# A one-core encoder layer with product-key experts: late picks for two tiles, a pinned row in the gather ring, and pools laid out from both ends

## The chip, the cores and the metric

The kernel runs on one core of a Trainium2 chip. Its engines are TensorE (PE in the rows), VectorE (DVE), ScalarE (ACT) and GpSimd (POOL); SyncE (SP) issues the plain DMAs, and GpSimd the gathers. Each engine works through its own instructions in their order. The metric is the device time of one execution in microseconds. Before the change it is 2861.89 us, the median of three runs (2860.47 to 2866.61).

## The reference

One layer over 1024 tokens of 1024 features: a token mixer, a layer of product-key experts, and a gated embedding. The change touches the experts (`P` is 128):

```python
def peer(n, w_q, sub_keys, expert_u, expert_v):
    q = (nf @ w_q).reshape(t, PEER_HEADS, D_KEY)             # 8 heads of 256
    s1 = jnp.einsum("thd,hkd->thk", q1, sub_keys[:, 0])      # 128 scores a side
    s2 = jnp.einsum("thd,hkd->thk", q2, sub_keys[:, 1])
    v1, i1 = lax.top_k(s1, TOPK)                             # 16 of 128
    v2, i2 = lax.top_k(s2, TOPK)
    cand = (v1[..., :, None] + v2[..., None, :]).reshape(t, PEER_HEADS, TOPK * TOPK)
    vals, ci = lax.top_k(cand, TOPK)
    idx = (e1 * N_KEYS + e2)                                 # 128 picks a token
    gates = jax.nn.softmax(vals, axis=-1)
    ...
        ug = expert_u[ib]                                    # 16384 experts of 1024
        act = jax.nn.gelu(jnp.einsum("td,tkd->tk", xb, ug)) * gb
        vg = expert_v[ib]
        return jnp.einsum("tk,tkd->td", act, vg)
h = h + peer(rmsnorm(h, g_ffn), ...)
gate = jax.nn.sigmoid(rmsnorm(h, g_ple) @ w_pg)
h = h + (p @ w_pe) * gate
return rmsnorm(h, g_final)
```

## The kernel before

The 1024 tokens are 8 tiles of 128. The **front** takes them in four pairs: the mixer (`mix_in`, `mix_out`), then `choose` (L283), which makes the queries and the scores of each head on TensorE, copies the scores with ScalarE, and has VectorE look for the 16 best (`top16`, L328, five instructions over 128 columns) and combine the two sides (`select`, L336: eight searches over 80 candidates, then one-hots over 1024 columns to read the keys). Between the heads `fill` (L319) takes the next pieces of the gate tables.

The experts are worked out in two ways. Tiles 1 to 4 (`DENSE`) go through all 16384 experts: `gate_table` (L395) turns picks and gates into a table of one gate per token and expert, by one-hots on VectorE, GpSimd and ScalarE and matmuls, and stores it to DRAM (`Wd`). The **dense stage** (`dense`, L436) then goes through 128 blocks of 128 experts: loads of u, v and the table's columns on SP; ScalarE rounds u and v to a short form (`uh`, `vh`), GpSimd makes the rest (`ul`, L470, `vl`, L477); 24 matmuls for z (L481 to L483); gelu; VectorE multiplies by the table (L486); three matmuls per output group and a sum on VectorE (L504 to L508). Tiles 5 to 7 (`GATHER`) fetch just the 128 picked rows of each token by indirect DMA: `u_step` (L524) gathers rows of expert_u (L536) into a ring of tiles `g`, and VectorE makes a dot with each (L538); `v_step` (L555) gathers rows of expert_v and adds them, weighted, to `accP` (L568). One step is 32 rows. Tile 0 (`MIXED`) has its u side gathered in the front and its v side in the dense stage, so it has a gate table too, made from its acts. One more step of 32, of tile 5, runs in the front (`UE`); the other gathers run beside and after the dense stage. The **back** (`back_in`, `back_out`) ends the layer tile by tile.

A scheduler sorts the instructions of all these loops into one order per engine from its own estimate of their times. Where a tile lies in SBUF is set by pools: the front's pools are closed at L641, and the dense stage's pools take over their space, tile by tile, as their last readers finish.

Four places matter here. `UAT, GAT` (L59) say after which pair tile 0's gathers and its table are put into the program: after the pair that begins with tile 6, the last one. `FG` is the front's ring of three `g` tiles; the normalized row that the dots are made with is a tile `hrow` of its own (L527). `choose` finds the picks of all eight tiles in the front. And `u`, `uh`, `ul` (pool `du`) lay in space that the gathers of the front didn't use.

Of the kernel before, what the change touches and what calls it, by code (L numbers as in the profile page):

```python
# [26 lines left out]
def trunk(ctx: ExitStack, tc: tile.TileContext, x, pT, w_inF, w_inV, chan, ln_c, w_sT, b_s, w_out, g_row,  # L27
# [7 lines left out]
    def row_const(pool, name, src, i, n):  # L35
# [23 lines left out]
    UAT, GAT, RATE = 6, 6, 3  # L59
# [7 lines left out]

    UE, WR = 1, 8
# [5 lines left out]
    nTd = dram.tile([P, 8, NA * P], F32, name="nTd")  # L74
    TG = 32
# [9 lines left out]
    wbp = fctx.enter_context(tc.tile_pool(name="wbp", bufs=2))  # L85
    psum = fctx.enter_context(tc.tile_pool(name="psum", bufs=2, space=bass.MemoryType.PSUM))

# [4 lines left out]
    iotaP = psum.tile([P, P], F32, name="iotaP", bufs=1)  # L92
# [190 lines left out]
    def choose(t0, nt, nT):  # L283
# [3 lines left out]
        for t in range(nt):  # L287
            tv = work.tile([P, 2, NH, K], F32, name="tv")
            ti = work.tile([P, 2, NH, K], U32, name="ti")
            top.append((tv, ti))  # L290
        for h in range(NH):
# [36 lines left out]
    def top16(v, i, s):  # L328
        nc.vector.max(v[:, 0:8], s)
        nc.vector.max_index(i[:, 0:8], v[:, 0:8], s)  # L330
        s2 = work.tile([P, s.shape[1]], F32, name="s2", bufs=4)
# [4 lines left out]
    def select(t, tv, ti):  # L336

        cand = work.tile([P, NH, 80], F32, name="cand", bufs=1)
        v1, v2 = tv[:, 0], tv[:, 1]
        nc.vector.tensor_add(cand[:, :, 0:16], v1[:, :, 0:1].to_broadcast([P, NH, 16]), v2)  # L340
        nc.vector.tensor_add(cand[:, :, 16:72].rearrange("p h (i j) -> p h i j", i=7),
                             v1[:, :, 1:8, None].to_broadcast([P, NH, 7, 8]),
                             v2[:, :, None, 0:8].to_broadcast([P, NH, 7, 8]))
        nc.vector.tensor_add(cand[:, :, 72:80], v1[:, :, 8:16], v2[:, :, 0:1].to_broadcast([P, NH, 8]))
        vals = work.tile([P, NH, K], F32, name="vals")
        pos = work.tile([P, NH, K], U32, name="pos")
        for h in range(NH):
            top16(vals[:, h], pos[:, h], cand[:, h])

        f = work.tile([P, 5, NH * K], BF, name="pf")  # L350
        p_ = pos.rearrange("p h k -> p (h k)")
        sh = work.tile([P, NH * K], U32, name="sh")
# [4 lines left out]
        ib = work.tile([P, 2, NH * K], BF, name="ib")  # L357
# [6 lines left out]
        own = work if t in GATHER else wbp  # L364
        e = own.tile([P, 2, NH * K], F32, name="e", bufs=2 if t in GATHER else 5)
        for side in range(2):
            for h0 in range(0, NH, HB):

                c = slice(h0 * K, (h0 + HB) * K)
                tb = work.tile([P, K, HB, K], BF, name="tb", bufs=1)  # L370
                nc.scalar.copy(tb, ti[:, side, h0:h0 + HB].rearrange("p h i -> p i h")[:, :, :, None]
                               .to_broadcast([P, K, HB, K]))
                oh = work.tile([P, K, HB * K], BF, name="oh", bufs=2)
                nc.vector.tensor_tensor(oh, iota16, ib[:, side, None, c].to_broadcast([P, K, HB * K]), op=OP.is_equal)
# [20 lines left out]
    def gate_table(t):  # L395
# [4 lines left out]
        pe = psum.tile([P, 4, P], F32, name="gt", bufs=3)  # L400
# [7 lines left out]
        for g in range(P // TG):  # L408
            st = wbp.tile([P, P, TG], F32, name="st")
            for q in range(0, TG, 4):  # L410
# [17 lines left out]
                pw = psum.tile([P, P, 4], F32, name="gt", bufs=3)  # L428
# [7 lines left out]
    def dense():  # L436
# [12 lines left out]
        def u_stage(b):  # L449
            if b % NG == 0:  # L450
# [4 lines left out]
                wm = dm.tile([P, P // TG, NG, TG], F32, name="wm")  # L455
# [94 lines left out]
    def experts(tiles):  # L550
# [185 lines left out]
```

## Time and profile before

| | us |
|---|---|
| median of three runs | 2861.89 |
| profiled execution | 2862.61 |
| its span | 2860.8 |
| PE, DVE, POOL, ACT busy | 2620.5, 2156.9, 1945.5, 1007.6 |
| last gate matmul of the front ends | 1084.29 |
| first matmul of the dense stage | 1086.52 |
| last gathered row added | 2830.14 |

The span is divided by the seam at 1086 us. Left of it all engines share the work and none is full; right of it PE is nearly full until the dense blocks end at about 2722 us, and from there to the end the last gathers and the back's matmuls run side by side. Matmuls are pipelined, so the busy time of PE is not matmuls times their mean. An idle time in square brackets is what the engine waited before that row, with what ended it.

### The profile page before, as it was taken

How to read it: one execution, taken by the hardware profiler on the slowest of the kernel's cores; microseconds unless marked ns; L12 is line 12 of the kernel's file. 1: busy time of each engine (PE TensorE's matmuls, PEld its weight loads, DVE VectorE, ACT ScalarE, POOL GpSimd, SP SyncE). 2: the span in 40 equal slices, each digit the busy share in tenths (PEclk: the TensorE clock that was granted, in tenths of full speed). 3: DMA queues.
4: the chain of work that ended last, by engine and by line, in shares of the span. 5: the costliest groups of instructions: out<-in, count | busy, mean ns of one | idle time of the engine just before them, and what ended most of it. 6: DMA issues, size and time to landing. Idle time of an engine off the chain costs nothing.

```text
span 2860.8 us, 37645 instructions
## 1 busy us (share of the span) xinstructions
PE 2620.5 (92%) x12671; PEld 2203.2 (77%) x12671; DVE 2156.9 (75%) x4738; ACT 1007.6 (35%) x1930; POOL 1945.5 (68%) x1740
## 2 busy tenths in 40 slices
PE   7998999889678678999999999999999999999988
PEld 6887888688677656888787888878787788788767
DVE  5567888999977886777777777777777777677776
ACT  3312455335764544222322223232222322222342
POOL 0000377347876787888878888888887878888773
PEclk9998999899789779999999999999999999999999
DMA  6353688787657649899999999999999999999885
GB/s 203 129 185 120 236 300 301 242 304 253 221 206 274 228 184 339 317 324 344 331 333 328 331 347 330 338 329 342 325 336 329 328 348 332 335 339 324 299 290 174
DMA packets 299698, 820.92 MB, mean 287 GB/s; under 512 B 26096, under 2 KB 117616, under 8 KB 296944
## 3 DMA queue, kind: packets, MB, share of 16 engines
q0 software_dynamic: 129024, 469.82, 45.8%
q1 hardware_dynamic: 170480, 348.70, 35.6%
q8 instruction: 100, 1.64, 0.2%
q14 instruction: 94, 0.77, 0.1%
HBM read 764.93 MB, written 53.48 MB: 286 GB/s over the span
## 4 chain that ended last, share of the span: by engine, by line
PE 33%; DMA 23%; DVE 17%; POOL 13%; issue 10%; ACT 2%; SPq 0%; POOLq 0%; DVEq 0%; ACTq 0%
DMA g<-expert_u,idx 10%; DMA g<-expert_v,idx 10%; PE z L158 4%; DVE g L538 4%; POOL g L536 4%; PE mm L612 3%; POOL vl L477 3%; PE mm L504 3%; PE z L481 3%; PE z L482 3%; PE mm L505 3%; PE mm L506 3%; PE z L483 3%; PE mm L299 2%; PE mm L267 2%
## 5 line engine op out<-in xcount | busy, mean ns | idle before, releaser
L536 POOL DMA_INDIRECT g<-expert_u,idx x512 | 511.9, 1000 | 369.6 <-DVE g L538 163.2
L568 DVE SCALAR_TENSOR_TENSOR accP<-g,act,accP 128x1024 f32<-128x1024 f32 x384 | 493.2, 1284 | 210.9 <-DMA g<-expert_v,idx 207.4
L538 DVE SCALAR_TENSOR_TENSOR g<-g,nP 128x1024 f32<-128x1024 f32 x352 | 422.8, 1215 | 178.5 <-DMA g<-expert_u,idx 177.1
L566 POOL DMA_INDIRECT g<-expert_v,idx x384 | 367.7, 957 | 144.4 <-DVE accP L568 60.7
L504 PE MATMUL mm<-vh,ah 128*128 128x512 f32 x1024 | 400.3, 392 | 13.5 <-DVE accA L508 6.8
L481 PE MATMUL z<-nh,uh 128*128 128x512 f32 x1024 | 401.8, 393 | 8.1 <-DVE al L490 5.9
L482 PE MATMUL z<-nl,uh 128*128 128x512 f32 x1024 | 400.6, 391 | 2.0 <-DVE nl L446 2.0
L483 PE MATMUL z<-nh,ul 128*128 128x512 f32 x1024 | 400.2, 391 | 0.0
L505 PE MATMUL mm<-vl,ah 128*128 128x512 f32 x1024 | 399.2, 391 | 0.0
L506 PE MATMUL mm<-vh,al 128*128 128x512 f32 x1024 | 396.7, 390 | 0.0
L421 POOL TENSOR_SCALAR oh<-iota,eT,gT 128x128 f32<-128x128 f32 x320 | 314.5, 991 | 63.9 <-PE gt L430 50.8
L468 ACT CAST uh<-u 128x1024 fp32r<-128x1024 f32 x128 | 134.8, 1053 | 574.8 <-PE z L482 459.3
L477 POOL TENSOR_TENSOR vl<-v,vh 128x512 fp32r<-128x512 f32 x256 | 328.2, 1302 | 3.2 <-ACT vh L475 0.7
L470 POOL TENSOR_TENSOR ul<-u,uh 128x1024 fp32r<-128x1024 f32 x128 | 309.3, 2417 | 6.9 <-ACT uh L468 4.6
L430 PE MATMUL gt<-oh,oh 128*128 128x128 f32 x1280 | 221.4, 321 | 95.1 <-POOL oh L421 40.4
L430 PEld LDWEIGHTS gt<-oh,oh 128*128 128x128 f32 x1280 | 194.5, 224 | 123.1 <-POOL oh L421 82.6
L475 ACT CAST vh<-v 128x512 fp32r<-128x512 f32 x256 | 153.1, 621 | 306.9 <-DMA v<-expert_v 250.6
L538 DVE SCALAR_TENSOR_TENSOR g<-g,hrow 128x1024 f32<-128x1024 f32 x160 | 197.3, 1236 | 72.3 <-DMA g<-expert_u,idx 72.2
L158 PE MATMUL z<-aT,w 128*128 128x256 f32 x960 | 227.0, 393 | 16.0 <-DMA w<-w_inF 13.1
L299 PE MATMUL mm<-nT,w 128*128 128x256 f32 x1024 | 237.0, 383 | 4.4 <-DMA w<-w_q 4.4
L508 DVE TENSOR_TENSOR accA<-mm,accA 128x512 f32<-128x512 f32 x320 | 217.8, 684 | 27.0 <-PE mm L506 26.7
L504 PEld LDWEIGHTS mm<-vh,ah 128*128 128x128 f32 x1024 | 193.0, 189 | 56.7 <-DVE accA L508 9.8
(368 smaller groups left out, 4586.6 us busy)
## 6 DMA issues: line engine op xcount, KB each, us to landing
u<-expert_uT SPq DMA_DIRECT2D x128, 512.0 KB, 6.4
v<-expert_v SPq DMA_DIRECT2D x128, 512.0 KB, 4.9
Wd<-st SPq DMA_DIRECT2D x20, 2048.0 KB, 8.4
w<-w_q SPq DMA_DIRECT2D x64, 512.0 KB, 4.8
w<-Wd SPq DMA_DIRECT2D x128, 256.0 KB, 9.7
w<-w_inF SPq DMA_DIRECT2D x60, 512.0 KB, 3.6
wo<-w_out SPq DMA_DIRECT2D x32, 512.0 KB, 4.5
g<-expert_u,idx POOLq DMA_INDIRECT x512, 6.3
```

Of the source, the lines that this page charges most:

```text
L430: nc.tensor.matmul(pw[:, :, k], oh2[:, k], oh1[:, k], start=True, stop=True)
L477: nc.gpsimd.tensor_tensor(vl, v[:, s * 512:s * 512 + 512], vh.bitcast(F32), op=OP.subtract)
L481: nc.tensor.matmul(ph, uh[:, c], nh[:, c], start=c == 0, stop=False)
L482: nc.tensor.matmul(ph, uh[:, c], nl[:, c], start=False, stop=False)
L483: nc.tensor.matmul(ph, ul[:, c], nh[:, c], start=False, stop=c == 7)
L504: nc.tensor.matmul(po, ah[:, c], vh, start=i == 0, stop=False)
L505: nc.tensor.matmul(po, ah[:, c], vl, start=False, stop=False)
L506: nc.tensor.matmul(po, al[:, c], vh, start=False, stop=i == NG - 1)
L536: nc.gpsimd.indirect_dma_start(out=ug, out_offset=None, in_=expert_u, in_offset=bass.IndirectOffsetOnAxis(ap=idx[:, k:k + 1], axis=0))
L538: nc.vector.scalar_tensor_tensor(ug, ug, 1.0, ns[t, front], op0=OP.mult, op1=OP.mult, accum_out=dots[:, k - b * KB:k - b * KB + 1])
L566: nc.gpsimd.indirect_dma_start(out=vg, out_offset=None, in_=expert_v, in_offset=bass.IndirectOffsetOnAxis(ap=idx[:, kk:kk + 1], axis=0))
L568: nc.vector.scalar_tensor_tensor(acc, vg, act[:, k:k + 1], acc, op0=OP.mult, op1=OP.add)
```

## The change

Seven edits belong together. (1) For tiles 6 and 7 (`LATE`) `choose` only stores the scores to DRAM (`sd`, 16 stores of 128 KB). `choose_late` loads them again, head by head into one buffer, and does searches and `select` on VectorE; it is called in `experts` ahead of the second steps of tiles 5 and 6. There the one-hots of `select` go over 256 columns in 16 rounds instead of 1024 in 4. (2) Tile 0's gathers and its table are put into the program after pair 3 (tiles 4 and 5) instead of pair 4. (3) The row h of the gathers has no tile of its own any more; it takes one of the `g` tiles and, in the front, holds it for as long as its tile's dots last. (4) `wbp`, `hold`, `gath`, `dm` and the new pool `late` are laid out from the right end of SBUF, the others from the left. The dense stage's `uh`, `ul` and the first `w` now lie over the front's `g` tiles. (5) `cand` is made for four heads at a time. (6) `wm` has one buffer instead of two. (7) The dense pools close after the expert steps instead of ahead of them, and the gate tables' PSUM is a pool of its own.

```diff
-    UAT, GAT, RATE = 6, 6, 3
+    UAT, GAT, RATE = 4, 4, 3
...
+    LATE = (6, 7)
...
+    sd = {t: dram.tile([P, NH, 2, P], F32, name=f"sd{t}") for t in LATE}
...
-    wbp = fctx.enter_context(tc.tile_pool(name="wbp", bufs=2))
+    wbp = fctx.enter_context(tc.tile_pool(name="wbp", bufs=2, side="right"))
...
             for t in range(nt):
+                if t0 + t in LATE:
+                    nc.sync.dma_start(sd[t0 + t][:, h], s[:, t])
+                    continue
                 tv, ti = top[t]
...
-            picks[t0 + t] = select(t0 + t, *top[t])
-
+            if t0 + t not in LATE:
+                picks[t0 + t] = select(t0 + t, *top[t])
+
+    def choose_late(t):
+
+        top = top_tiles()
+        for h in range(NH):
+            s = sel.pool.tile([P, 2, P], F32, name="s")
+            nc.sync.dma_start(s, sd[t][:, h])
+            for side in range(2):
+                top16(top[0][:, side, h], top[1][:, side, h], s[:, side])
+        picks[t] = select(t, *top)
...
+    class Sel:
+
+        def __init__(self, pool, heads, bufs):
+            self.pool, self.heads, self.bufs = pool, heads, bufs
+            self.iota = (pool if bufs else fconst).tile([P, K, heads * K], BF, name="iota16", bufs=1)
...
+    sel = Sel(work, 4, None)
...
-                wm = dm.tile([P, P // TG, NG, TG], F32, name="wm")
+                wm = dm.tile([P, P // TG, NG, TG], F32, name="wm", bufs=1)
...
-            h = gath.tile([P, D], F32, name="hrow", bufs=1)
+            h = gath.tile([P, D], F32, name="g")
...
         prev = None
+        late = list(LATE)
         for st in steps:
+            if late and st[1] == 1:
+                choose_late(late.pop(0))
             if st not in acts:
...
-    hold = ctx.enter_context(tc.tile_pool(name="hold", bufs=1, reuse_waits="tile"))
-    gath = ctx.enter_context(tc.tile_pool(name="gath", bufs=BG, reuse_waits="tile"))
+    hold = ctx.enter_context(tc.tile_pool(name="hold", bufs=1, side="right", reuse_waits="tile"))
+    gath = ctx.enter_context(tc.tile_pool(name="gath", bufs=BG, side="right", reuse_waits="tile"))
...
-    dm = dctx.enter_context(tc.tile_pool(name="dm", bufs=2, reuse_waits="tile"))
+    dm = dctx.enter_context(tc.tile_pool(name="dm", bufs=2, side="right", reuse_waits="tile"))
+    late = dctx.enter_context(tc.tile_pool(name="late", bufs=1, side="right", reuse_waits="tile"))
+    sel = Sel(late, 1, 1)
     dense()
+    h_last = experts(GATHER)
     dctx.close()
-    h_last = experts(GATHER)
```

What the scheduler makes of it shows at three places at the seam. GpSimd before, the first two `ul` (L470), among the gate one-hots (L421) of tile 4:

```order
L421 TENSOR_SCALAR oh2_6679<-iota_122,eT_6333,gT_6332 128x128 [waits PE_49]
L421 TENSOR_SCALAR oh2_6679<-iota_122,eT_6333,gT_6332 128x128 x3
L470 TENSOR_TENSOR ul_8718<-u_8714,uh_8716 128x1024 [waits DMAHW4_49,DMAHW3_49,DMAHW5_49,DMAHW2_49,DMAHW6_49,DMAHW1_49,DMAHW7_49,DMAHW0_49,Activation_49]
L470 TENSOR_TENSOR ul_8765<-u_8761,uh_8763 128x1024 [waits DMAHW2_49,DMAHW1_49,DMAHW4_49,DMAHW0_49,Activation_49]
L421 TENSOR_SCALAR oh2_6709<-iota_122,eT_6333,gT_6332 128x128 [waits PE_49]
L421 TENSOR_SCALAR oh2_6709<-iota_122,eT_6333,gT_6332 128x128 x3
```

GpSimd after, the same two (L499 now; L565 is a gather, `g_19525` and above are those of tile 5's second step):

```order
L565 DMA g_19567<-expert_u,idx_5826 128x1024 [waits DMASW6_49,DVE_49]
L576 TENSOR_TENSOR act_8245<-act_8245,gate_5819 128x32 [waits Activation_49]
L565 DMA g_19570<-expert_u,idx_5826 128x1024 [waits DMASW7_49,DVE_49]
L565 DMA g_19573<-expert_u,idx_5826 128x1024 [waits DMASW0_49,DVE_49]
L565 DMA g_19576<-expert_u,idx_5826 128x1024 [waits DMASW1_49,DVE_49]
L565 DMA g_19579<-expert_u,idx_5826 128x1024 [waits DMASW2_49,DVE_49]
L565 DMA g_19582<-expert_u,idx_5826 128x1024 [waits DMASW3_49,DVE_49]
L499 TENSOR_TENSOR ul_8347<-u_8343,uh_8345 128x1024 [waits DMAHW3_49,Activation_49]
L565 DMA g_19585<-expert_u,idx_5826 128x1024 [waits DMASW4_49,DVE_49]
L499 TENSOR_TENSOR ul_8394<-u_8390,uh_8392 128x1024 [waits DMAHW4_49,Activation_49]
```

The first `ul` has moved behind the last gate one-hot and 28 gathers that follow it.

SP before, the first loads of the table's columns (`w`, L453) and of u (L466), among the query weights `w3`:

```order
L453 DMA w_8703<-Wd1_92 128x4x128 [waits DMAHW2_49,DMAHW5_49,DMAHW0_49,PE_49]
L453 DMA w_8703<-Wd2_93 128x4x128
L453 DMA w_8703<-Wd3_94 128x4x128
L466 DMA u_8714<-expert_uT 128x1024
L466 DMA u_8761<-expert_uT 128x1024
L453 DMA w_8902<-Wd1_92 128x4x128 [waits DMAHW3_49,DMAHW1_49]
L453 DMA w_8902<-Wd2_93 128x4x128
L453 DMA w_8902<-Wd3_94 128x4x128
L434 DMA Wd4_95<-st_6484 128x4096 [waits DMAHW4_49,Activation_49]
```

SP after (L482 and L495 now; L325 are the score loads of tile 6's pick, L485 and L501 the loads of `wm` and v):

```order
L485 DMA wm_8536<-Wd0_98 128x4x128 [waits DMAHW6_49,DMAHW3_49,Pool_49]
L325 DMA s_19224<-sd6_92 128x256 [waits DMAHW4_49,DMAHW0_49,DVE_49]
L485 DMA wm_8875<-Wd0_98 128x4x128 [waits DMAHW5_49,DMAHW3_49,Pool_49]
L325 DMA s_19238<-sd6_92 128x256 [waits DMAHW4_49,DVE_49]
L482 DMA w_8332<-Wd1_94 128x4x128 [waits DMAHW7_49,DVE_49]
L482 DMA w_8332<-Wd2_95 128x4x128
L482 DMA w_8332<-Wd3_96 128x4x128 [waits DMAHW1_49]
L482 DMA w_8332<-Wd4_97 128x4x128 [waits DMAHW2_49]
L495 DMA u_8343<-expert_uT 128x1024
L495 DMA u_8390<-expert_uT 128x1024
```

The u loads stand behind score loads that wait on VectorE, and behind a `w` load that waits on it too.

VectorE before, what follows the last gate one-hot (L423): the lower part of the tokens (`nl`, L446) and the first dots of tile 5's second step:

```order
L423 TENSOR_SCALAR oh2_8509<-iotaP_124,eT_8088,gT_8087 128x128 [waits Pool_49]
L423 TENSOR_SCALAR oh2_8509<-iotaP_124,eT_8088,gT_8087 128x128 x3
L531 TENSOR_TENSOR nP_19559<-nP_19559,g_ffn_77 128x1024 [waits Activation_49]
L446 TENSOR_TENSOR nl_8670<-al_8671,nh_8669 128x512 [waits DMAHW4_49,Activation_49]
L446 TENSOR_TENSOR nl_8670<-ah_8675,nh_8669 128x512 [waits DMAHW5_49,Activation_49]
L538 SCALAR_TENSOR_TENSOR g_19563,dots_19562<-g_19563,nP_19559 128x1024 [waits DMASW0_49,DVE_49]
L538 SCALAR_TENSOR_TENSOR g_19566,dots_19562<-g_19566,nP_19559 128x1024 [waits DMASW1_49]
L538 SCALAR_TENSOR_TENSOR g_19569,dots_19562<-g_19569,nP_19559 128x1024 [waits DMASW2_49]
```

VectorE after, some 50 rows behind the last gate one-hot (L357 to L362 are the searches, L372 and L375 `cand`, L567 the dots; `g_8242` is the last gather of tile 5's front step):

```order
L358 MAX_INDEX ti_19181<-tv_19180,s_19224 128x8 [waits DVE_49]
L372 TENSOR_TENSOR cand_19296<-tv_19180 128x4x56
L567 SCALAR_TENSOR_TENSOR g_8239,dots_8148<-g_8239,g_8144 128x1024 [waits DMASW7_49]
L361 MAX tv_19180<-s2_19228 128x8 [waits DVE_49]
L362 MAX_INDEX ti_19181<-tv_19180,s2_19228 128x8 [waits DVE_49]
L375 TENSOR_TENSOR cand_19296<-tv_19180 128x4x8
L567 SCALAR_TENSOR_TENSOR g_19552,dots_19524<-g_19552,nP_19521 128x1024 [waits DMASW0_49]
L360 MATCH_REPLACE s2_19234<-tv_19180,s_19224 128x128 [waits DVE_49]
L567 SCALAR_TENSOR_TENSOR g_8242,dots_8148<-g_8242,g_8144 128x1024 [waits DMASW1_49]
L361 MAX tv_19180<-s2_19234 128x8 [waits DVE_49]
L567 SCALAR_TENSOR_TENSOR g_19555,dots_19524<-g_19555,nP_19521 128x1024 [waits DMASW2_49]
```

The dots of the front's last step now stand between the searches of tile 6's pick; from the last one-hot to `g_8242` there are 18 dots and nearly four heads.

## Rows read from the trace of the kernel before

**Rows 1.** The page, busy us of an engine, its share of the span, instructions.

```profile
PE 2620.5 (92%) x12671; PEld 2203.2 (77%) x12671; DVE 2156.9 (75%) x4738; ACT 1007.6 (35%) x1930; POOL 1945.5 (68%) x1740
```

**Rows 2.** Stretches: busy us (instructions) by engine; PE clock, DMA share, GB/s.

```profile
500.00:600.00 100.00, 83.95 (x470) 71.76 (x470) 92.83 (x337) 31.53 (x58) 33.09 (x31) 0.86 0.78 265
700.00:800.00 100.00, 76.90 (x494) 69.55 (x493) 94.89 (x369) 67.22 (x162) 82.69 (x78) 0.85 0.68 236
840.00:1086.00 246.00, 183.52 (x957) 159.22 (x955) 190.41 (x687) 130.38 (x302) 181.26 (x192) 0.82 0.62 224
1086.00:1546.00 460.00, 444.89 (x1910) 364.54 (x1911) 332.67 (x452) 134.33 (x208) 373.07 (x311) 0.97 0.95 334
...
2724.00:2861.00 137.00, 118.41 (x523) 96.01 (x521) 98.44 (x103) 46.94 (x81) 76.98 (x89) 0.94 0.66 227
```

**Rows 3.** DVE lines kept apart by shape: as section 5 of the page.

```profile
L330 DVE FIND_INDEX8 ti<-tv,s 128x8 uint32<-128x128 f32 x128 | 35.9, 282 | 0.0
...
L332 DVE MATCH_REPLACE8 s<-tv,s 128x128 f32<-128x128 f32 x128 | 34.9, 273 | 0.0
...
L374 DVE TENSOR_TENSOR oh<-iota,ib 128x1024 bf16<-128x1024 bf16 x32 | 21.7, 688 | 0.0
...
L330 DVE FIND_INDEX8 pos<-vals,cand 128x8 uint32<-128x80 f32 x64 | 14.4, 231 | 0.0
...
L330 DVE MATCH_VALUE_LOAD ti<-tv,s 128x8 f32 x128 | 9.8, 76 | 0.0
```

**Rows 4.** Section 5 of the page: group | busy us, mean ns | idle.

```profile
L538 DVE SCALAR_TENSOR_TENSOR g<-g,hrow 128x1024 f32<-128x1024 f32 x160 | 197.3, 1236 | 72.3 <-DMA g<-expert_u,idx 72.2
```

**Rows 5.** POOL in time, 562 to 600 us: start, length, row, [idle, releaser].

```profile
562.40 1.94 POOL L536 DMA_INDIRECT g<-expert_u,idx  x1 [0.15 <-DVE s L332]
...
600.05 1.15 POOL L536 DMA_INDIRECT g<-expert_u,idx  x1 [0.84 <-DVE g L538]
```

**Rows 6.** POOL in time, 820 to 980 us.

```profile
826.44 0.28 POOL L547 TENSOR_TENSOR wm<-wm,gate 128x32 f32<-128x32 f32 x1
...
839.14 0.56 POOL L122 TENSOR_TENSOR rB<-ss,half 128x1 f32<-128x1 f32 x1 [1.46 <-DVE ss L119]
...
847.72 1.07 POOL L536 DMA_INDIRECT g<-expert_u,idx  x1 [1.85 <-DVE idx L392]
...
968.69 1.03 POOL L536 DMA_INDIRECT g<-expert_u,idx  x1 [0.17 <-issue]
...
978.04 5.64 POOL L470 TENSOR_TENSOR ul<-u,uh 128x1024 fp32r<-128x1024 f32 x2
```

**Rows 7.** PE in time, end of the front and first dense blocks.

```profile
1082.34 1.95 PE L430 MATMUL gt<-oh,oh 128*128 128x128 f32 x14 [0.37 <-DVE oh L423]
1086.52 0.73 PE L481 MATMUL z<-nh,uh 128*128 128x512 f32 x2 [2.23 <-ACT nh L445]
...
1109.63 1.22 PE L504 MATMUL mm<-vh,ah 128*128 128x512 f32 x2 [6.55 <-ACT vh L475]
```

**Rows 8.** The page, sections 5 and 6 (issues: count, KB each, us to landing).

```profile
L421 POOL TENSOR_SCALAR oh<-iota,eT,gT 128x128 f32<-128x128 f32 x320 | 314.5, 991 | 63.9 <-PE gt L430 50.8
L468 ACT CAST uh<-u 128x1024 fp32r<-128x1024 f32 x128 | 134.8, 1053 | 574.8 <-PE z L482 459.3
...
L470 POOL TENSOR_TENSOR ul<-u,uh 128x1024 fp32r<-128x1024 f32 x128 | 309.3, 2417 | 6.9 <-ACT uh L468 4.6
...
u<-expert_uT SPq DMA_DIRECT2D x128, 512.0 KB, 6.4
```

**Rows 9.** The chain of waits, 840 to 1130 us: start, length, what.

```profile
1093.04 15.90 DMA v<-expert_v
```

**Rows 10.** POOL lines of 2724 to 2861 us.

```profile
L566 POOL DMA_INDIRECT g<-expert_v,idx x43 | 45.0, 1046 | 23.2 <-DVE accP L568 16.3 <-issue 6.0 <-DVE sg L620 0.6
```

**Rows 11.** DVE in time, end of the gathers.

```profile
2828.86 1.28 DVE L568 SCALAR_TENSOR_TENSOR accP<-g,act,accP 128x1024 f32<-128x1024 f32 x1
```

**Rows 12.** PE in time, transposes of the last tile.

```profile
2836.08 1.03 PE L594 MATMUL z<-ident,a 128*128 128x128 f32 x8
```

More of the change, by code (lines that the diff above doesn't have):

```diff
@@ L287, in choose @@
         for t in range(nt):
-            tv = work.tile([P, 2, NH, K], F32, name="tv")
-            ti = work.tile([P, 2, NH, K], U32, name="ti")
-            top.append((tv, ti))
+            if t0 + t not in LATE:
+                top.append(top_tiles())
         for h in range(NH):
@@ L314, in choose, with top_tiles, tile @@
         for t in range(nt):
[L315 removed]
+            if t0 + t not in LATE:
+                picks[t0 + t] = select(t0 + t, *top[t])
[7 more added lines that the diff above has]
+        picks[t] = select(t, *top)
+    def top_tiles():
+        return sel.tile([P, 2, NH, K], F32, "tv"), sel.tile([P, 2, NH, K], U32, "ti")
+    class Sel:
+        def __init__(self, pool, heads, bufs):
+            self.pool, self.heads, self.bufs = pool, heads, bufs
+            self.iota = (pool if bufs else fconst).tile([P, K, heads * K], BF, name="iota16", bufs=1)
+            nc.gpsimd.iota(self.iota, pattern=[[1, K], [0, heads * K]], base=0, channel_multiplier=0,
+                           allow_small_or_imprecise_dtypes=True)
+        def tile(self, shape, dt, name, bufs=2):
+            return self.pool.tile(shape, dt, name=name, bufs=self.bufs or bufs)
+    sel = Sel(work, 4, None)
     filler, n_gt = [], [0]
@@ L330, in top16 @@
         nc.vector.max_index(i[:, 0:8], v[:, 0:8], s)
-        s2 = work.tile([P, s.shape[1]], F32, name="s2", bufs=4)
+        s2 = sel.tile([P, s.shape[1]], F32, "s2", 4)
         nc.vector.match_replace(s2, v[:, 0:8], s, NEG)
@@ L336, in select @@
     def select(t, tv, ti):
[L338 to L350, printed above, removed]
+        vals = sel.tile([P, NH, K], F32, "vals")
+        pos = sel.tile([P, NH, K], U32, "pos")
+        for h0 in range(0, NH, 4):
+            cand = sel.tile([P, 4, 80], F32, "cand")
+            v1, v2 = tv[:, 0, h0:h0 + 4], tv[:, 1, h0:h0 + 4]
+            nc.vector.tensor_add(cand[:, :, 0:16], v1[:, :, 0:1].to_broadcast([P, 4, 16]), v2)
+            nc.vector.tensor_add(cand[:, :, 16:72].rearrange("p h (i j) -> p h i j", i=7),
+                                 v1[:, :, 1:8, None].to_broadcast([P, 4, 7, 8]),
+                                 v2[:, :, None, 0:8].to_broadcast([P, 4, 7, 8]))
+            nc.vector.tensor_add(cand[:, :, 72:80], v1[:, :, 8:16], v2[:, :, 0:1].to_broadcast([P, 4, 8]))
+            for h in range(4):
+                top16(vals[:, h0 + h], pos[:, h0 + h], cand[:, h])
+        f = sel.tile([P, 5, NH * K], BF, "pf")
         p_ = pos.rearrange("p h k -> p (h k)")
-        sh = work.tile([P, NH * K], U32, name="sh")
+        sh = sel.tile([P, NH * K], U32, "sh")
         nc.vector.tensor_scalar(sh, p_, 3, None, op0=OP.logical_shift_right)
@@ L356, in select @@
         nc.vector.scalar_tensor_tensor(f[:, 1], f[:, 0], -64.0, f[:, 1], op0=OP.add, op1=OP.max)
-        ib = work.tile([P, 2, NH * K], BF, name="ib")
+        ib = sel.tile([P, 2, NH * K], BF, "ib")
         nc.vector.tensor_copy(ib[:, 0], f[:, 1])
@@ L363, in select @@
         nc.vector.tensor_add(ib[:, 1], f[:, 4], f[:, 3])
-        own = work if t in GATHER else wbp
-        e = own.tile([P, 2, NH * K], F32, name="e", bufs=2 if t in GATHER else 5)
+        e = sel.tile([P, 2, NH * K], F32, "e") if t in GATHER else wbp.tile([P, 2, NH * K], F32, name="e", bufs=5)
+        HB = sel.heads
         for side in range(2):
@@ L556, in v_step @@
             if b == 0:
-                h = gath.tile([P, D], F32, name="hrow", bufs=1)
+                h = gath.tile([P, D], F32, name="g")
                 nc.sync.dma_start(h, h1d[t])
@@ L569, in v_step @@
             if b == P // KB - 1:
-                h = gath.tile([P, D], F32, name="hrow", bufs=1)
+                h = gath.tile([P, D], F32, name="g")
                 nc.scalar.copy(h, acc)
```

19 lines of the change are left out of this document (8 added, 11 removed).

## The prediction

> **What bounds the kernel now.** I read the summary of engines first, then busy time by stretch, then single engines in order of time around the seams. TensorE is busy 92% of the span [rows 1], but not evenly. In the dense stage it has little to give: 444.89 of 460 us from 1086 to 1546, with VectorE at 332.67 [rows 2]. So the dense stage ends when TensorE has done its matmuls, and whatever moves its start moves the end. The front is another matter. At 500 to 600 and 700 to 800 us VectorE is busy 92.83 and 94.89 us of 100, TensorE only 83.95 and 76.90 [rows 2]: there the picks, the one-hots and the gathered dots on VectorE are late. From 840 to 1086 VectorE has 190.41 of 246 us and TensorE 183.52, at a granted clock of 0.82 [rows 2]; neither is full. The profiled run took 2862.61 us, 1.8 more than its span of 2860.8 and 0.7 more than the median of 2861.89. The sum is made against the profiled run.
>
> **What leaves the front.** A pick of one tile is 16 searches over 128 columns and 8 over 80. A search has five instructions of 273 to 282 ns and three value loads of 76 [rows 3], 1.61 us; over 80 columns five of 231 and the loads, 1.38. That is 16 × 1.61 + 8 × 1.38 = 36.8 us. The one-hot part has eight passes at 688 ns [rows 3], 5.5 us, and halvings, which I estimate at 4.5 more: 47 us a tile, 94 for both, gone from VectorE in the front. How much of it shows depends on what is late next. Two things replace it: the matmuls of pair 4 and of the gate tables, which stay, and the ring of gathers. The ring still has three slots, but now the pinned row h sits in one: two are free. With three, 14 gathers from 562.40 to 600.05 [rows 5] make 13 intervals of 2.90 us, a slot's round being 8.69 us (issue, landing, dot, and the wait for VectorE to come to it). With two the same round gives one gather per 4.34 us.
>
> I take the last piece of the front, from pair 4's norm to the last gate matmul. Before, it runs from 839.14 + 0.56 [rows 6] to 1082.34 + 1.95 [rows 7], 244.6 us. After, GpSimd's order has 33 groups of gate one-hots and 47 gathers there (before 38 and 32). By the ring 47 × 4.34 = 204 us. By GpSimd alone 33 × 4 × 0.991 [rows 8] + 47 × 1.05 (1.03 to 1.07 [rows 6]) = 180. The later of the two holds: 244.6 − 204 = **−40 us**, from −64 (GpSimd alone) to 0 (the ring also delays what stands before it; the earlier pairs I take as unmoved, since they lose dots and get a slower ring).
>
> **What the seam costs.** Before, the first two lower parts of u, `ul`, were made at 978.04 us [rows 6], a hundred us ahead of their matmuls, and TensorE went from the last gate matmul to the first dense one with 2.23 us idle; one more wait, 6.55 us for vh at 1109.63, followed [rows 7]. After, `uh`, `ul` and the first w lie over the slots of the front's ring. The first w load waits on VectorE, the first u load stands behind it on SP's queue, and on GpSimd 28 gathers stand between the last gate one-hot and the first `ul`. What they all wait for is VectorE: between its last one-hot and the last dot of tile 5's front step it has 18 dots and four heads of tile 6's pick. 18 × 1.236 [rows 4] + 4 × 2 × 1.61 = 35 us, with two small adds 36. Behind that come the u load 6.4, the cast 1.053 and the subtraction 2.417 [rows 8]: 9.9. At a VectorE that never waits the gap is 46 us. From 840 to 1086 it was busy 77% (190.41 of 246), and here it waits for landings again, and for the score loads, which share one buffer: 36 / 0.77 = 47, the gap 57. Two waits of before, 2.23 + 6.55, fall inside. Added: **+48 us**. Below: 46 − 8.8 = +37. Above: a busy share of 0.6 and a first load as slow as the first v, 15.90 us [rows 9]: 60 + 19.4 − 8.8 = +71. The gap can't hide: both products of a block need `uh`, the third needs `ul`, and no gate matmuls are left.
>
> **What the dense stage takes up.** The two picks become 94 us plus about 8 for the one-hot passes in eighths instead of halves, over the first 460 us, where VectorE had 460 − 332.67 = 127 us free [rows 2]. It would be busy at 435 of 460, 94%. That is the load of 700 to 800 us, where TensorE lost much; but there its matmuls were fed by VectorE directly, and here two buffers of z lie between. From 0 (127 is more than 102) to 60 (TensorE at 83.95 of 100, the 500 to 600 row, instead of 96.7: 13% of 460). I take a third, **+20 us**, nearer to the row of the same stage.
>
> Here the Trainium skill has a rule that speaks against the change. The row: GpSimd is busy 373.07 of the 460 us [rows 2], 87 free. The rule (SBUF — State Buffer, Who interferes with whom): a VectorE instruction with two inputs in SBUF and a GpSimd instruction that reads SBUF shut each other out for a whole instruction. The searches' replacing and index steps have two such inputs, as do `ul` and `vl`. If a quarter of the 102 us fell on GpSimd's work, some 25 of its 87 free us would go; it would still keep up, so by that rule the sum stays, with less room. No row here shows such a block apart.
>
> **The end.** Ten more gathers of the expert steps are placed ahead of the last dense blocks: 49 are left after it instead of 59. In 2724 to 2861 us GpSimd spent 45.0 + 23.2 us on 43 [rows 10], 1.6 each: 16 us. But TensorE's own back is nearly as late: the last gather is added at 2828.86 + 1.28 [rows 11] and the last tile's transposes start at 2836.08 [rows 12]. Half of it: **−8 us**, from −16 to 0.
>
> **Sum.** 2862.6 − 40 + 48 + 20 − 8 = 2882.6; less the 0.7 to the median, **2882 us**.
>
> **Rivals.**
> 1. *VectorE alone was late in the front.* Two slots are enough, since a slot's round shrinks when VectorE comes to it sooner, and all 94 us go. For it: 94.89 of 100 at 700 to 800 us [rows 2]. Against: from 840 on, where most of tile 7's pick stood, VectorE had 55 us idle. 2862 − 94 + 48 + 20 − 8 = 2828. It decides from a round of 7 us (47 × 3.5 = 165).
> 2. *The ring takes the whole gain.* Rounds of two slots hold the 128 gathers of tile 0 as well, and pair 4 starts later by what its own stretch saves. For it: 2.90 against 4.34 us. Against: tile 0's acts, done at 826.44 [rows 6], took longer per gather than that before too. 0 + 48 + 20 − 8: 2922.
> 3. *The picks slow every block.* VectorE at 94% holds TensorE as in the front: +60 for +20, 2922. For it: the rows of 500 to 800 us. Against: the free 127 us.
> 4. *The terms cancel*, with a seam of 37 us and +5 in the dense stage: −40 + 37 + 5 − 4 = −2, 2860.
>
> The change does what it says in each: the order has the searches behind the last one-hot.
>
> **How the numbers follow.** My forecast has 40%, with its own range from 2868 to 2905. Rival 1 has 28%, rival 2 13%, rival 3 9%, rival 4 10%. This kernel's times tell 0.2%, 5.7 us, from no change. Faster: rival 1, 28%. Within: rival 4, 10%. Slower: 40 + 13 + 9 = 62%. The range of 2830 to 2928 leaves out the lower half of rival 1 and a few in a hundred above.
>
> **What would show it.** Right: a TensorE idle time near 50 us, released by GpSimd's `ul`, ahead of the first dense product; GpSimd's gathers of tile 0 at over 4 us each; VectorE at over 90% from the seam on for about 400 us; the front's last gate matmul at 1030 to 1055. Wrong: that matmul before 1010 (rival 1) or after 1075 (rival 2), a seam under 20 us, or a dense stage whose TensorE is busy under 90% in its first 460 us (rival 3).

## The result

The changed kernel takes 2985.52 us (median of four runs, 2978.71 to 2992.45) against 2861.18: a ratio of 1.0431, interval 1.0403 to 1.0459. The forecast was 2882 with a range up to 2928: the sign was right and the size was not. The profiled execution took 2992.45 us, its span is 2990.7. Where the 130 us between the two spans went:

| | before | after | difference | forecast |
|---|---|---|---|---|
| last gate matmul ends | 1084.3 | 1088.0 | +3.7 | −40 |
| from there to the first dense matmul | 2.2 | 75.6 | +73.3 | +55 |
| dense stage, first to last matmul | 1636.3 | 1693.9 | +57.6 | +13 |
| from there to the last row of VectorE | 134.3 | 129.6 | −4.7 | −8 |

(The forecast's +48 for the seam is split here into the gap, 57 us instead of 2.2, and the 6.6 us wait for vh, which lay behind the first dense matmul.)

Busy time by stretch of the changed kernel (columns as in [rows 2]; the last two stretches begin at its first dense matmul and at the end of its dense stage):

```profile
500.00:600.00 100.00, 79.65 (x464) 68.98 (x465) 94.54 (x336) 36.98 (x70) 30.20 (x30) 0.91 0.72 237
700.00:800.00 100.00, 76.60 (x451) 67.50 (x450) 84.92 (x332) 65.33 (x156) 75.15 (x74) 0.86 0.59 206
840.00:1088.00 248.00, 171.66 (x894) 151.41 (x894) 130.78 (x247) 107.71 (x256) 177.16 (x185) 0.82 0.63 225
1163.60:1623.60 460.00, 412.94 (x1701) 330.48 (x1702) 431.27 (x887) 125.06 (x203) 320.16 (x265) 0.95 0.85 286
2857.50:2991.00 133.50, 119.08 (x536) 97.00 (x534) 86.85 (x93) 46.87 (x81) 66.00 (x80) 0.95 0.56 199
```

From 840 to 1088 us VectorE has lost 60 us of work and stands idle almost half of the time; GpSimd works about as much as before, TensorE 12 us less [rows 2], and the stretch is no shorter. In the dense stage VectorE comes to 431 of 460 us (435 were forecast, but by other terms, see below), and TensorE falls from 444.89 [rows 2] to 412.94.

GpSimd in time: the gathers of tile 0 on their own (answering [rows 5]), and its last act (answering [rows 6]).

```profile
562.42 0.94 POOL L565 DMA_INDIRECT g<-expert_u,idx  x1 [4.64 <-DVE g L567]
...
590.55 0.94 POOL L565 DMA_INDIRECT g<-expert_u,idx  x1 [2.86 <-DVE g L567]
...
959.53 0.62 POOL L576 TENSOR_TENSOR wm<-wm,gate 128x32 f32<-128x32 f32 x1
```

Between the first two rows lie eight intervals, 3.52 us each: two free slots, so a round of 7.0. Over all 128 gathers of tile 0 it is 4.96 us (before 3.92), and the last act comes at 959.53 instead of 826.44. Between pair 4's norm and the last gate matmul there are 46 gathers 5.32 us apart, a round of 10.6. They reach from end to end of the stretch, but that alone does not show that the ring sets its length: before, with three slots, 37 gathers lay 5.62 us apart there.

TensorE at the seam (answering [rows 7]):

```profile
1084.22 3.82 PE L459 MATMUL gt<-oh,oh 128*128 128x128 f32 x16 [3.50 <-POOL oh L450]
1163.59 0.79 PE L510 MATMUL z<-nh,uh 128*128 128x512 f32 x1 [75.55 <-ACT uh L497]
```

What the 75.55 us consist of shows on three engines in time. VectorE (L567 are the dots; L560 makes the row for tile 5's second step):

```profile
1089.70 1.97 DVE L567 SCALAR_TENSOR_TENSOR g<-g 128x1024 f32<-128x1024 f32 x1 [3.75 <-DMA g<-expert_u,idx]
...
1104.62 4.77 DVE L567 SCALAR_TENSOR_TENSOR g<-g 128x1024 f32<-128x1024 f32 x1 [8.29 <-DMA g<-expert_u,idx]
...
1120.99 1.23 DVE L560 TENSOR_TENSOR nP<-nP,g_ffn 128x1024 f32<-128x1024 f32 x1 [8.70 <-ACT nP L559]
...
1144.75 1.22 DVE L567 SCALAR_TENSOR_TENSOR g<-g 128x1024 f32<-128x1024 f32 x1
```

SP (L482 and L495 are the loads of `w` and u):

```profile
1144.86 0.34 SPq L325 DMA_DIRECT2D s<-sd  x1
1146.00 2.69 SPq L482 DMA_DIRECT2D w<-Wd  x4
1148.74 2.96 SPq L495 DMA_DIRECT2D u<-expert_uT  x2
```

ScalarE, the rounding of u (L497):

```profile
1162.49 1.04 ACT L497 CAST uh<-u 128x1024 fp32r<-128x1024 f32 x1 [16.25 <-DMA u<-expert_uT]
```

The last dot of tile 5's front step ends at 1145.97 us. Three hundredths later SP issues the `w` load, behind it u; u lands 13.7 us later (its median before was 6.4 [rows 8]), and only then `uh` starts. The links forecast for the gap are all there but one (`uh` ends it, and `ul` costs 1.22 us more behind it); the waits in them were longer.

What TensorE waited for in the first 460 us of the dense stage, first after (engine, tile, line <- releaser: us, times, longest):

```profile
PE mm L533 <- DVE accA L537: 41.8, 20, 4.8
PE mm L533 <- ACT ah L517: 1.9, 2, 1.1
```

And the same before:

```profile
PE mm L504 <- DVE accA L508: 6.0, 3, 2.2
```

TensorE waits for VectorE to add a finished output group, and the late picks stand ahead of that addition. The longest of these waits stand behind one-hot passes of `select` that took several times their usual time. One shape of them, in the front before (first row) and in those 460 us after:

```profile
L377 DVE TENSOR_TENSOR oh<-oh 128x128 bf16<-128x128 bf16 x32 | 7.1, 221 | 0.2
L406 DVE TENSOR_TENSOR oh<-oh 128x128 bf16<-128x128 bf16 x30 | 20.9, 697 | 0.5
```

And the longest of TensorE's waits, with two such passes ahead of the addition and what GpSimd did meanwhile:

```profile
1286.47 2.36 POOL L499 TENSOR_TENSOR ul<-u,uh 128x1024 fp32r<-128x1024 f32 x1
1286.56 2.37 DVE L406 TENSOR_TENSOR oh<-oh 128x128 bf16<-128x128 bf16 x1
1289.45 1.85 DVE L406 TENSOR_TENSOR oh<-oh 128x64 bf16<-128x64 bf16 x1
1289.96 1.28 POOL L506 TENSOR_TENSOR vl<-v,vh 128x512 fp32r<-128x512 f32 x1
1291.95 0.80 PE L533 MATMUL mm<-vh,ah 128*128 128x512 f32 x1 [4.79 <-DVE accA L537]
```

Of the 192 late one-hot passes 37 took over 0.3 us more than the quickest of their shape, 72 us together. Each of the 37 overlapped a subtraction (`ul`, `vl` or `ml`) on GpSimd, and none of the other 155 did. In all six of TensorE's waits over 3 us in these 460, an instruction of `select` that was held up in this way stands within the 3 us before the wait, or in it.

### The profile page after: what moved, and what is told of

It is laid out like the page before. It is cut to its first block, busy times and chain, and to the rows that moved or that the text cites. A ratio compares the mean times of both kernels' runs of the same rounds, so it can differ in the third digit from the quotient of the medians.

```text
span 2990.7 us, 37907 instructions
## 1 busy us (share of the span) xinstructions
PE 2628.0 (88%) x12671; PEld 2203.8 (74%) x12671; DVE 2264.1 (76%) x4906; ACT 1012.1 (34%) x1956; POOL 1935.7 (65%) x1741
## 4 chain that ended last, share of the span: by engine, by line
PE 30%; DVE 21%; DMA 20%; POOL 13%; issue 13%; ACT 2%; SPq 0%; POOLq 0%; DVEq 0%; ACTq 0%
DMA g<-expert_u,idx 11%; DMA g<-expert_v,idx 5%; DVE g L567 5%; POOL oh L450 4%; POOL g L565 3%; DVE accP L597 3%; PE mm L533 3%; PE z L158 3%; PE mm L535 3%; PE mm L534 3%; PE z L510 3%; PE z L511 3%; PE z L512 3%; PE mm L644 3%; POOL vl L506 2%
## 5 line engine op out<-in xcount | busy, mean ns | idle before, releaser
L565 POOL DMA_INDIRECT g<-expert_u,idx x512 | 506.7, 990 | 417.1 <-DVE g L567 190.3
L567 DVE SCALAR_TENSOR_TENSOR g<-g,nP 128x1024 f32<-128x1024 f32 x352 | 423.9, 1214 | 171.4 <-DMA g<-expert_u,idx 164.0
L533 PE MATMUL mm<-vh,ah 128*128 128x512 f32 x1024 | 407.9, 399 | 46.3 <-DVE accA L537 43.8
L499 POOL TENSOR_TENSOR ul<-u,uh 128x1024 fp32r<-128x1024 f32 x128 | 308.2, 2408 | 22.4 <-ACT uh L497 20.3
L567 DVE SCALAR_TENSOR_TENSOR g<-g 128x1024 f32<-128x1024 f32 x160 | 202.5, 1266 | 146.3 <-DMA g<-expert_u,idx 146.0
L497 ACT CAST uh<-u 128x1024 fp32r<-128x1024 f32 x128 | 134.7, 1052 | 526.1 <-PE z L511 303.5
L510 PEld LDWEIGHTS z<-nh,uh 128*128 128x128 f32 x1024 | 193.2, 189 | 128.4 <-ACT uh L497 75.8
```

The source lines that it names most:

```text
L510: nc.tensor.matmul(ph, uh[:, c], nh[:, c], start=c == 0, stop=False)
L533: nc.tensor.matmul(po, ah[:, c], vh, start=i == 0, stop=False)
L565: nc.gpsimd.indirect_dma_start(out=ug, out_offset=None, in_=expert_u, in_offset=bass.IndirectOffsetOnAxis(ap=idx[:, k:k + 1], axis=0))
L567: nc.vector.scalar_tensor_tensor(ug, ug, 1.0, ns[t, front], op0=OP.mult, op1=OP.mult, accum_out=dots[:, k - b * KB:k - b * KB + 1])
```

## The experiments

Twelve kernels ran. In the table, times in the middle are from each profiled execution: tile 0's last act, last gate matmul, first and last dense matmul, and gathers issued after that. Each ratio is over the kernel before as it ran beside that kernel (medians 2857.77 to 2861.18), so it is not the quotient of two rows.

| kernel | median us | ratio (interval) | act | gate | dense | left |
|---|---|---|---|---|---|---|
| before | 2861.18 | 1 | 826 | 1084 | 1087 to 2723 | 43 |
| after | 2985.52 | 1.0431 (1.0403–1.0459) | 960 | 1088 | 1164 to 2857 | 33 |
| e1_ring4 | 2923.43 | 1.0234 (1.0198–1.0271) | 801 | 1089 | 991 to 2739 | 68 |
| e2_gathF_right | 2969.14 | 1.0379 (1.0340–1.0418) | 953 | 1106 | 990 to 2791 | 60 |
| e3_nopick | 2919.56 | 1.0205 (1.0170–1.0241) | 955 | 1084 | 1157 to 2781 | 33 |
| e4_before_ring2 | 2924.57 | 1.0223 (1.0188–1.0258) | 932 | 1082 | 1152 to 2791 | 9 |
| e5_nolate | 2919.29 | 1.0231 (1.0205–1.0257) | 951 | 1083 | 1151 to 2783 | 34 |
| e7_ring4_nolate | 2880.83 | 1.0093 (1.0066–1.0121) | 810 | 1103 | 1050 to 2699 | 68 |
| e8_ring4_late7 | 2908.75 | 1.0194 (1.0168–1.0220) | 806 | 1102 | 1012 to 2729 | 68 |
| e9_before_uat4 | 2867.86 | 1.0045 (1.0023–1.0066) | 804 | 1093 | 1095 to 2723 | 43 |
| e10_onering | 2866.50 | 1.0033 (1.0014–1.0051) | 736 | 1097 | 1055 to 2729 | 47 |
| e11_onering_late | 2917.94 | 1.0210 (1.0182–1.0238) | 737 | 1085 | 985 to 2777 | 49 |
| e12_onering_acc | 2866.43 | 1.0022 (1.0004–1.0040) | 738 | 1100 | 1059 to 2725 | 47 |
| e14_ring4_thirds | 2917.50 | 1.0208 (1.0159–1.0258) | 812 | 1078 | 1022 to 2742 | 69 |

**One more slot in the front's ring** (of the changed kernel):

```diff
-    FG, BG = 3, 5
+    FG, BG = 4, 5
```

> The changed kernel with one more tile in the front's gather ring: three free slots beside the pinned row, as before the change. Theory A (two free slots held the front, and pushed tile 5's front gathers over the seam): tile 0's last act comes near 830 us instead of 960, the first dense matmul near 1010 to 1050 instead of 1164, its idle time ahead of it under 15 us instead of 76, and the total is 2850 to 2885 us, with the dense stage still some 60 us longer than before the change. Theory B (the front is held by TensorE and by the one-hots on GpSimd; the ring only follows): the act stays near 960 or the front's end near 1085, and the total stays above 2910.

The act and the idle time came as theory A says, the total did not. TensorE in time, its first dense matmul:

```profile
991.40 0.50 PE L510 MATMUL z<-nh,uh 128*128 128x512 f32 x1 [0.59 <-ACT uh L497]
```

62 us came back. The dense blocks now start among the last gate groups, but the dense stage still ends 16 us after that of before, and 68 gathers are left instead of 43, which lengthens the end.

**The front's ring laid elsewhere** (of the changed kernel):

```diff
-    gath = fctx.enter_context(tc.tile_pool(name="gathF", bufs=FG))
+    gath = fctx.enter_context(tc.tile_pool(name="gathF", bufs=FG, side="right"))
```

> The changed kernel with the front's gather ring laid out from the right end, so that the dense stage's u, its rounded part and its lower part no longer lie over it; two free slots and the late picks stay. If the overlap made the seam: TensorE's idle time of 76 us ahead of the first dense matmul falls under 15, the front's last gate matmul stays at 1080 to 1095, the dense stage stays some 60 us longer, total 2910 to 2925. If the searches on VectorE made it wherever u lies: idle stays above 45 us, total above 2955.

TensorE's first dense matmul in this kernel:

```profile
990.49 0.79 PE L510 MATMUL z<-nh,uh 128*128 128x512 f32 x1 [1.62 <-ACT uh L497]
```

The overlap made the idle time: without it 1.62 us are left, although the dots of tile 5's front step are about as late as in the changed kernel (its act comes at 1142.49 us, there at 1146.79). The total missed what I expected, since only 16 us came back (28 between the two profiled executions): the last dense matmul is 66 us earlier, but 60 gathers are left after it and the end is 38 us longer.

**The picks left out** (the body of `choose_late`):

```diff
-        top = top_tiles()
...
-        picks[t] = select(t, *top)
+        picks[t] = picks[5]
```

> The changed kernel without the late picks: tiles 6 and 7 gather by the picks of tile 5, so that the loads of scores, the searches and the selection of both tiles are left out. If VectorE's picks slow the dense blocks: the 62 us that the first 33 blocks lose go, and 10 to 20 us of the seam (four heads' searches, 13 us), total 2905 to 2925. If the loss in the dense stage has another cause (one buffer for the tile 0 table, pools closed later): it stays within 15 us of 62, total above 2960.

TensorE's first dense matmul:

```profile
1156.62 0.79 PE L504 MATMUL z<-nh,uh 128*128 128x512 f32 x1 [73.12 <-ACT uh L491]
```

Busy time in the 460 us from there (columns as in [rows 2]):

```profile
1156.60:1616.60 460.00, 454.52 (x1978) 372.63 (x1979) 332.81 (x451) 127.17 (x195) 376.02 (x312) 0.99 0.94 332
```

The dense stage is back at 1624 us with VectorE at 332.81: its loss is the picks. But of the seam only 2.4 us go: the searches stood in waits that were there anyway.

**The ring of before cut to two** (of the kernel before):

```diff
-    FG, BG = 3, 5
+    FG, BG = 2, 5
```

> The kernel before the change with a front ring of two tiles instead of three, its row h still in a tile of its own. Theory A (the ring sets the pace of tile 0's gathers): 4.3 to 5 us a gather instead of 4.1, last act of tile 0 near 930 to 960 instead of 826, total 2920 to 2980. Theory B (TensorE and GpSimd hold the front): last act within 30 us of 826, total under 2880.

TensorE's first dense matmul:

```profile
1151.50 1.22 PE L481 MATMUL z<-nh,uh 128*128 128x512 f32 x2 [69.13 <-ACT nh L445]
```

4.85 us a gather, an act at 932 and +65 us, as theory A has it. The last gate matmul did not move, however (1082): what two slots cost shows as an idle time of 69 us at the seam, in a kernel with no late picks and none of the new layout. The link is another there: `nh` on ScalarE starts right behind the act of tile 5's front step, which waits for the last of its dots.

**The picks back in the front** (of the changed kernel):

```diff
-    LATE = (6, 7)
+    LATE = ()
```

> The changed kernel with the picks of tiles 6 and 7 back in the front (the list of late tiles empty); the ring of two free slots, the layout and tile 0 ahead of pair 4 stay. If the ring alone sets the front's end, the relief of VectorE was worth nothing there: tile 0's last act stays at 950 to 975 us, the last gate matmul at 1080 to 1095, the seam's idle time at 60 to 80, the dense stage falls back to 1625 to 1645, total 2915 to 2935. If VectorE's relief was worth part of the 94 us: last act and last gate matmul 20 to 60 us later, total 2940 to 2985.

Busy time at the front's end and in the first 460 us of the dense stage:

```profile
840.00:1083.00 243.00, 180.11 (x893) 154.92 (x892) 193.70 (x692) 111.03 (x255) 182.58 (x184) 0.78 0.62 215
1150.50:1610.50 460.00, 449.83 (x1948) 368.76 (x1949) 331.71 (x448) 126.63 (x194) 370.15 (x306) 0.98 0.93 329
```

VectorE has its 63 us back in the front, and the front ends 5 us sooner, not later. With two slots the relief was worth nothing there. Seam 67.79, dense 1632.6: the late picks alone cost 66 us.

**Three free slots, no late picks** (both edits):

```diff
-    FG, BG = 3, 5
+    FG, BG = 4, 5
...
-    LATE = (6, 7)
+    LATE = ()
```

> The changed kernel with three free slots in the front's ring and no late picks: what is left of the change is the layout from both ends and tile 0 ahead of pair 4. If the ring and the picks in the dense stage are the whole loss: the dense stage starts early (first dense matmul before 1085, idle under 15 us), takes VectorE no more than before, and the total is 2845 to 2870. If the layout or the order of tile 0 has a cost of its own: above 2885.

Between the two bounds. The dense stage ends 24 us before that of the kernel before, but the end gives more than that back. GpSimd's gathers from the end of the dense stage on (answering [rows 10]):

```profile
L595 POOL DMA_INDIRECT g<-expert_v,idx x64 | 66.0, 1031 | 36.1 <-DVE accP L597 23.4 <-issue 6.1 <-DMA g<-expert_v,idx 3.3
```

Four more of expert_u make the 68. In GpSimd's order 26 fewer gathers stand ahead of the last `ul` than before (802 against 828): the dense stage's gather ring lies over the gate tables' tiles, and no gather was issued between 982 and 1116 us.

**Only tile 7's picks late** (of e1_ring4):

```diff
-    LATE = (6, 7)
+    LATE = (7,)
...
-            if late and st[1] == 1:
+            if late and st == (6, 1):
```

> The changed kernel with three free slots in the front's ring and only tile 7's picks late. If the cost of late picks goes by VectorE's time in the dense stage, half of it is left: total 2880 to 2900, between the kernel without late picks and the 2923 of both, gathers left after the last dense block 50 to 60 (43 before the change, 68 with both late). If the first tile's picks made the loss, by standing at the start of the dense stage: within 10 us of the kernel without late picks.

28 us over the kernel without late picks, of 43 for both tiles, and 68 gathers left: total and gathers lie outside what I expected of half the cost. It is not nothing; with intervals of 7 to 10 us on each kernel, half (21 us) is not excluded.

**Tile 0 ahead of pair 4, alone** (of the kernel before):

```diff
-    UAT, GAT, RATE = 6, 6, 3
+    UAT, GAT, RATE = 4, 4, 3
```

> The kernel before the change with tile 0's gathers and table put into the program after pair 3 instead of pair 4, and nothing else. If that order is worth nothing by itself, since the gathers are paced by the ring and by VectorE: 2850 to 2870. If it is what the front's gain would come from: 2815 to 2840.

As expected: that order gains nothing (0.45% slower). Tile 0's act comes 22 us sooner and the last gate matmul 9 us later.

**One ring of five for the whole program** (no late picks; room from four small selection tiles in one buffer):

```diff
+    gath = ctx.enter_context(tc.tile_pool(name="gath", bufs=BG, side="right", reuse_waits="tile"))
     fctx = ExitStack()
...
-    gath = fctx.enter_context(tc.tile_pool(name="gathF", bufs=FG))
```

> The changed kernel without late picks and with one gather ring of five tiles for the whole program, at the right end of SBUF (some small tiles of the selection in one buffer instead of two make room): in the front four slots are free beside the pinned row, and the dense stage's gathers no longer lie over the gate tables' tiles. With three free slots and no late picks the last dense block ended 24 us earlier than before the change, but 68 gathers were left after it instead of 43. If that tail was made by the gathers that were ordered late, behind the gate tables: fewer than 55 are left, the tail is 130 to 150 us, the total 2835 to 2855, faster than before the change. If the tail is held by memory traffic whatever the order: the tail stays at 165 to 180, the total at 2870 to 2890.

Half right: 47 gathers are left and the end is 138 us, but the dense stage ends later by 30 us, and the total is 2866. What TensorE waited for from 1050 to 1300 us, first row:

```profile
PE mm L533 <- ACT vh L504: 25.8, 2, 24.5
```

**The same with the late picks** (of e10_onering):

```diff
-    LATE = ()
+    LATE = (6, 7)
```

> The same one ring of five, with the late picks of tiles 6 and 7 as in the change: the change with its ring mended. If the dense stage's loss goes by VectorE's load: first dense matmul near 990 to 1010, dense blocks 50 to 65 us longer than before the change over the first 36, total 2865 to 2900, slower than the same without late picks by 30 to 50. If only the ring was at fault: within 10 us of the same without late picks.

The late picks cost 51 us here; the total lies above the range I gave.

**Two loads moved** (of e10_onering; the same lines are taken out where they stood):

```diff
         def u_stage(b):
+            v = dv.tile([P, D], F32, name="v")
+            nc.sync.dma_start(v, expert_v[b * P:(b + 1) * P])
...
         for b in range(NG):
             u_stage(b)
+        for i, t in enumerate(TABLE):
+            nc.sync.dma_start(accA[:, i], h1d[t])
```

> The kernel with one gather ring of five and no late picks, with two loads moved: v is loaded at the head of a block's stage instead of behind the tile 0 table, and the loads of the tokens' sums (accA) come after the first four blocks' loads. There TensorE waited 24.5 us for the first vh, because v stood on SP's queue behind accA loads that wait for the last gate matmul. If that queue is the cause: this wait falls under 14 us, the dense stage ends near 2715, the total is 2845 to 2858 against 2860 before the change. If memory traffic at the seam is: the wait stays over 20 us and the total at 2862 to 2872.

The same wait in this kernel:

```profile
PE mm L533 <- ACT vh L504: 20.8, 4, 10.4
```

The longest wait fell to 10.4 us, the sum only to 20.8, and the total stayed at 2866. No version here beats the kernel before.

**Gate one-hots in thirds** (on e1_ring4):

```diff
-                    if n_gt[0] % 2:
+                    if n_gt[0] % 3 == 1:
...
-                    elif t == MIXED:
+                    elif t == MIXED or n_gt[0] % 3 == 2:
```

> The changed kernel with three free slots in the front's ring, and the gate one-hots dealt out in thirds: of every three groups one goes to GpSimd, one to VectorE, one to ScalarE (VectorE for tile 0), instead of every other one to GpSimd. In every kernel so far, with and without late picks and with two to four free slots, the 320 groups of gate matmuls kept one pace (65 by 600 us, 197 to 213 by 900) and ended at 1083 to 1103 us. If that chain of groups holds the front's end, and VectorE's time freed by the late picks could pay for it: over 215 groups by 900 us, the last gate matmul before 1070, the dense stage's end 15 to 50 us ahead of the 2739 of the same kernel with halves. If the order of the program or TensorE holds the pace: groups by 900 us within 6 of 199, dense end within 10 of 2739.

Inconclusive. By 900 us there are 213 groups (199 in e1_ring4, counted alike) and the last gate matmul comes at 1078, 11 us sooner, which leans to the chain of groups; but neither reaches the bound named (215, 1070), and the dense stage still ended at 2742, as the other theory has it. What holds the last gate matmul at 1078 to 1106 us in all fourteen kernels, with tile 0's acts done anywhere from 736 to 960, is not settled.

## Why the prediction was wrong

**The front, −40 forecast, +4 measured.** The step that failed is "The later of the two holds: 244.6 − 204": that the front's last piece is over when the ring or GpSimd's own work is. Its price was off too. The round of 8.69 us was read where GpSimd did nothing but gather; there it was even shorter after the change, 7.0 us (3.52 us a gather, rows above), as rival 1 wanted. In the stretch of the sum, between groups of one-hots in GpSimd's order, the gathers are 5.32 us apart instead of 4.34. But neither term sets the end. With two slots instead of three the last gate matmul of the kernel before comes at 1082 us instead of 1084; with the picks put back into the front, that of the changed kernel comes 5 us sooner. Where more slots are free, late picks bring it forward by 14 and 11 us (e1_ring4 against e7_ring4_nolate, e11_onering_late against e10_onering), far from 40. In e1_ring4 no gather is issued between 965 and 1101 us, and the last gate matmul still comes at 1089 (the dense stage's work already stands among the gate groups there, so this kernel alone would not decide). So what holds the front's end stays open; the runs show that the two things I had it depend on, VectorE's load and the ring's slots, brought it forward by 14 us at most. The part of rival 2 that delays pair 4 did not come either: its norm is at 845 us, before 839.

**The seam, a gap of 57 us forecast, 75.6 measured.** Where it lies and behind what (last dot, `w`, u, `uh`) was right; that GpSimd's `ul` would release TensorE was not, `uh` did. The step that failed is the price: "36 / 0.77". I worked it out from VectorE's work, four heads and 18 dots, as if VectorE were the one late. From its last one-hot to the last dot are 60 us, in which VectorE waits 20.7 (3.75, 8.29 and 8.70 in the rows above), about twice what the 0.77 gives. The run without picks has nearly the same idle time (73.12), and the kernel before with two slots has 69.13 without any of the change's seam. So it is the late dots of tile 5's front step, waiting for landings (8.29) and for the row of the second step (8.70), and the slow u load, 13.7 us. The late dots cost this only where the dense stage waits for them: in e2_gathF_right they are as late, and TensorE starts at 990 us. The upper bound, 60 + 19.4 = 79 us of gap, held.

**The dense stage, +20 forecast; +58 measured, 64 without the wait for vh that went.** Rival 3's mechanism at nearly its price of 60. The step that failed is "I take a third". I let the 127 us of free time count as cover; but TensorE needs VectorE at certain times, once in every output group, and the waits for its addition grew from 6.0 to 41.8 us in the first 460. These waits are the larger part of what was lost there, not all of it: the granted clock is 0.95 instead of 0.97. A term under it was mis-sized as well. I had 28 us for the one-hot part of both tiles (5.5 + 4.5 for each, and 8); the 192 passes took 113, of which 72 are time held up, so "by that rule the sum stays" was wrong too. It was not the searches that were held, as I had it: their index and replacing steps took 283 and 274 ns in those 460 us, as in the front before (282 and 273 [rows 3]). That VectorE's total still came out near 435 is luck. Leaving the picks out gave 69.5 us back in the dense stage (1693.9 to 1624.4), putting them into the front 61. The other kernels with both picks late lost 67 to 70 us in held passes, the one with tile 7's alone 36, those with the picks in the front next to nothing; but no run has the searches late without the passes, so how the loss divides between them is not shown.

**The end, −8 forecast, −4.7 measured:** right, with ten gathers fewer left (33 for 43).

So the front's term of rival 2 (the gathers of tile 0 were held as it says, pair 4 was not late) and rival 3 came together, which I had priced as alternatives, and with them a gap near the top of its range. Between kernels: two slots instead of three cost 65 us in the kernel before (e4_before_ring2), 62 in the changed one (over e1_ring4) and 38 in the changed one without late picks (e5_nolate over e7_ring4_nolate); the late picks cost 43 to 66 in four pairs (e1_ring4 over e7_ring4_nolate, e11_onering_late over e10_onering, the changed kernel over e5_nolate and e3_nopick). 62 + 43 + the 20 of e7_ring4_nolate over the kernel before are the 124 measured, but by construction, since the kernels between cancel; taken in the other order, the same two edits are 66 and 38.

## What to carry to other kernels

Work moved off an engine gains only where that engine ends the wait: first find what paces the stretch, then move (here 94 us taken off VectorE brought the front's end forward by 14 us at most, and what holds it is still open). A ring's round is to be read in the stretch where it will decide, with what else stands in the issuing engine's order; and a pinned tile in a ring counts as one slot less from the first instruction on. A tile that lies over a ring waits for the ring's last reader (75.55 us of idle time, 1.62 with the ring elsewhere). An instruction does not take the same time in another stretch: one shape with two inputs in SBUF took 221 ns in the front and 697 in the mean beside GpSimd's subtractions. Free time of a helper is not cover when its in-order queue puts the new work ahead of something the bound engine needs every block.

## What was not expected of the hardware

A dot with both inputs in SBUF took 4.77 us at 1104.62 (row above) instead of 1.22, while GpSimd ran four subtractions back to back:

```profile
1103.39 4.91 POOL L506 TENSOR_TENSOR vl<-v,vh 128x512 fp32r<-128x512 f32 x4
```

The dot ended at 1109.39, 1.1 us after them: it was held until the run of four was over. The Trainium skill (SBUF — State Buffer, Who interferes with whom) says that a VectorE instruction with two SBUF inputs and a GpSimd instruction that reads SBUF block each other for a whole instruction; the trace agrees that one waits, and shows that the wait can last over several instructions: 3.5 us, where each of the four took about 1.26. It need not: 15 us earlier, in another run of four, a dot begun at 1089.70 took 1.97 us, and the second subtraction then took 2.25. I had left this rule without a price in the prediction; the held one-hot passes above fit it too, and they cost 72 us of VectorE's time. In the front of the kernel before the same passes went free: 82 of their 192 overlapped one of GpSimd's gate one-hots, and none took 0.3 us more than the quickest of its shape. There GpSimd was the one that waited: its one-hots have a median of 1.13 us where a VectorE instruction with two SBUF inputs overlapped them, and 0.79 where none did.
